# Pricing the planner from the trace: a two-layer hybrid trunk on one core

## The chip, the cores and the metric

The kernel runs on one core of one Trainium2 chip. Its time is device microseconds of one launch. Three runs of the kernel before took 2161.36, 2166.35 and 2168.34 us; the median is 2166.35 us. One further execution was taken by the hardware profiler and is the source of every row below.

## The reference

Two layers act on 512 tokens of width 1024, all in f32:

```python
for i in range(2):
    x = layer_norm(ALPHA*x + 0.5*swiglu(x, ffn1...))          # width 2816
    x = layer_norm(ALPHA*x + hybrid_mixer(x, positions, ...))
    ffn = 0.5*swiglu(x, ffn2...)
    ple = sigmoid(x @ ple_w_gate) * (p[i] @ ple_w_proj)
    x = layer_norm(ALPHA*x + ffn + ple)
```

`hybrid_mixer` projects x to 12 groups of columns and runs three kinds of heads beside each other: four of retention (rotary angles, decay by distance, a state per chunk), a gated linear recurrence over 384 channels behind a causal convolution of width 4, and six of gated delta rule (convolution, SiLU, unit-norm q and k, per chunk a triangular system, a state carried from chunk to chunk). Their outputs, normed and gated, meet in `w_out`.

## The kernel before

All matmuls of weights are split: an f32 operand is rounded to a high part (ScalarE, `act`), the residue is its low part (VectorE, `tt` with SUB), and three products of 128 rows by 256 or 512 columns replace one. All of these go through `mm` (L305). The feed-forward stages take their gate and up matrices by a scheme of seven block products in place of eight (`Unit`), in 256-column matmuls; the down matrices, `w_out` and the embedding use 512-column ones (`rows`). Weights come by DMA on SP's queue into four `raw` tiles; `step_one` splits the next ones ahead of use, up to 14 us of matmul time ahead (`TARGET`) in the feed-forward stages and 5 us in the mixer. In part of them the residue is made by an accumulating DMA that POOL issues (L436, `add_one`), once ScalarE has written the negated weight.

The order of everything is decided while the program is written, by a planner on the host. It keeps a clock for each engine, P, D, A and G for TensorE, VectorE, ScalarE and GpSimd (L218 to L256 and L692 state their prices in ns), and for every 64 elements of a tile the time at which they are ready. `spend` (called by every helper) adds an instruction's price to its engine's clock, behind its inputs, with a hop of 110 ns between engines.

Side work is written as generators, so-called threads: `norm` (layer norm and transposes; these are marked urgent), `decays`, `delta` (one per pair of heads and half of the tokens: normalise k, build the triangular matrix, six levels of its inverse, two rounds of refinement, states, output norm), `lru`, `turn` and `retention`, and `blocks`/`combine` for the sums of the seven-product scheme. After every main matmul `poll` looks at each thread:

```python
if th.t + HOP <= clk["P"] and (th.urgent or max(clk["D"], clk["A"]) <= p + BACKLOG) and not th.done:
    step(th)
```

So a thread's next step (some transposes or small matmuls and what VectorE, ScalarE and GpSimd do with them) is placed in the engines' queues once its last result is ready by the planner's clocks, and only while neither D nor A is more than `BACKLOG` ahead of P. `wait_until` steps threads, earliest first, when the main line can't go on: for a PSUM bank, or for free slots in SBUF. In the mixer `unit` does the main work: it waits for three free slots (five before a rotated block), takes weights, runs 24 matmuls of 512 columns, and convolves, rotates or applies a function. The blocks come in the order q (3), x (3), l (3), r (4), z (3), g (2), after the k and v blocks; each q block spawns a `delta` of the second half. Hardware queues run strictly in the order that results.

`either(ns_v, ns_g)` (L223) gives a product to GpSimd when that clock, plus ns_g, is earlier than VectorE's plus ns_v; the mixer's weight residues use it with 70 + 1.04 n against 90 + 2.0 n, masks with 600 against 1110. `pmm` and `ptr` are side matmuls and transposes, with prices given at each call (58, 107, 215 and others).

Of the kernel before, what the change touches and what calls it, by code (L numbers as in the profile page):

```python
# [25 lines left out]
TARGET = 14.0  # L26
LEVELS = (2, 4, 8, 16, 32, 64)
HOP = 110.0
BACKLOG = 1800.0
GUARD = 6  # L30
ROOM_D = 4
ROOM_1, ROOM_2, ROOM_3, ROOM_O, ROOM_R = 5, 4, 3, 2, 5
# [77 lines left out]
def tile_trunk(ctx: ExitStack, tc: tile.TileContext, a, out):  # L110
# [28 lines left out]
    def blocks(ap):  # L139
        per = ap.ap[0][0]  # L140
        lo = ap.offset % per
        hi = lo + sum((n - 1) * abs(k) for k, n in ap.ap[1:])
        name = ap.tensor.name
        return [(name, i) for i in range(lo // 64, hi // 64 + 1)]

    def available(e, ins):
        t = 0.0
        for ap in ins:
            for b in blocks(ap):
                if b in ready:  # L150
                    f, g = ready[b]
                    t = max(t, f + (60.0 if g == e else HOP))
        return t

    def place(e, t, ns):

        if e == "P" or INORDER:
            clk[e] = max(clk[e], t) + ns
            return clk[e]
        q = gaps[e]  # L160
        for i, (g0, g1) in enumerate(q):
            s = max(g0, t)
            if s + ns <= g1:
                del q[i]
                if g1 - s - ns > 50.0:
                    q.insert(i, (s + ns, g1))
                if s - g0 > 50.0:
                    if len(q) == q.maxlen:
                        q.popleft()
                        i -= 1  # L170
                    q.insert(max(i, 0), (g0, s))
                return s + ns
        s = max(ends[e], t)
        if s - ends[e] > 50.0:
            q.append((ends[e], s))
        ends[e] = s + ns
        return s + ns
# [13 lines left out]
    def spend(e, ns, outs=(), ins=()):  # L191
        c = cur[0]
        t = place(e, max(c.t0, available(e, ins)), ns)
        for ap in outs:
            for b in blocks(ap):
                ready[b] = (t, e)
        if e != "P":
            clk[e] = max(clk[e], t)
        if not lazy[0]:
            c.t = max(c.t, t)  # L200
        emitted[0] += 1
# [5 lines left out]
    def size(ap):  # L207
        n = 1
        for d in ap.shape[1:]:
            n *= d  # L210
        return n
# [3 lines left out]

    def act(out, in_, func=AF.Copy, **kw):
        nc.scalar.activation(out=out, in_=in_, func=func, **kw)  # L217
        ns = 60 + 0.833 * size(out) + 90 * len(kw)  # L218
        if tables.get(func, table[0]) != table[0]:
            table[0] = tables[func]  # L220
            ns += 1280
        spend("A", ns, [out], [in_] + [v for v in kw.values() if not isinstance(v, float)])
# [4 lines left out]

    def ew(eng, ns, n, out, *ins):
        if eng is nc.gpsimd:
            spend("G", 90 + 2.0 * n, [out], ins)  # L230
        else:
            spend("D", ns + 1.04 * n, [out], ins)

    def tt(out, in0, in1, op, eng=None):
        (eng or nc.vector).tensor_tensor(out=out, in0=in0, in1=in1, op=op)  # L235
        ew(eng, 70, size(out), out, in0, in1)

    def stt(out, in0, scalar, in1, op0, op1):
        nc.vector.scalar_tensor_tensor(out=out, in0=in0, scalar=scalar, in1=in1, op0=op0, op1=op1)  # L239
        ew(None, 100, size(out), out, in0, in1, *([] if isinstance(scalar, float) else [scalar]))  # L240

    def ts(out, in0, s1, op0, s2=None, op1=None, eng=None):
        if op1 is None:
            (eng or nc.vector).tensor_scalar(out=out, in0=in0, scalar1=s1, scalar2=None, op0=op0)  # L244
        else:
            (eng or nc.vector).tensor_scalar(out=out, in0=in0, scalar1=s1, scalar2=s2, op0=op0, op1=op1)
        ew(eng, 100, size(out) * 0.6, out, in0, *[x for x in (s1, s2) if x is not None and not isinstance(x, float)])

    def cp(out, in_, eng=None):
        (eng or nc.vector).tensor_copy(out=out, in_=in_)  # L250
        ew(eng, 70, size(out), out, in_)

    def rsum(out, in_):
        nc.vector.tensor_reduce(out=out, in_=in_, axis=AX.X, op=ALU.add)
        ew(None, 70, size(in_), out, in_)

    def pmm(out, lhsT, rhs, ns, start=True, stop=True):

# [7 lines left out]
    def step(th):  # L266
        keep = cur[0]
        cur[0] = th
        th.t0 = clk["P"]
        try:  # L270
            next(th.gen)
        except StopIteration:
            th.done = True
            side.remove(th)
        cur[0] = keep
# [7 lines left out]
    def poll():  # L283
        p = clk["P"]
        for th in list(side):
            if th.t + HOP <= clk["P"] and (th.urgent or max(clk["D"], clk["A"]) <= p + BACKLOG) and not th.done:
                step(th)
# [89 lines left out]
    for l in range(L):  # L377
        gu_at["ln_ffn1", l] = add_gu(l, a["wgu1"], GROUP)
        add_rows(a["ffn1_w_down"][l], MT)
        for c in (0, 804, 1608):  # L380
            n = min(804, 2144 - c)
# [63 lines left out]
    def low(hi, lo, w, dma, j):  # L445
        if dma and not any(th.urgent for th in side):
            act(lo, w, scale=-1.0)
            readers[j] += 1
            adds.append((cur[0].t, lo, w, j))
            cur[0].t += 6000.0  # L450
        else:
            tt(lo, w, f32(hi), SUB)
# [8 lines left out]
    def step_one():  # L461
# [7 lines left out]
        if c == "plain":  # L469
            w = ra[:, 0:n]  # L470
            hi = slots.get([128, 1024], F32R)
            lo = slots.get([128, 1024], F32R)
            act(hi[:, 0:n], w)
            tt(lo[:, 0:n], w, f32(hi[:, 0:n]), SUB, either(70 + 1.04 * n, 90 + 2.0 * n) if in_mixer[0] else None)
            readers[j] -= 1
            o = new_op((j,), [hi, lo], [("plain", hi, lo)], 5.4)
        elif c in ("P1", "P2"):
# [3 lines left out]
            for s in (slice(0, 512), slice(512, 1024)) if st["step"] < 3 else (slice(0, 1024),):  # L481
                act(hi[:, s], w[:, s])
                low(hi[:, s], lo[:, s], w[:, s], n, j + int(c == "P2"))
# [15 lines left out]
        elif c == "B2b":  # L499
            hi, lo = sums.pop(j)  # L500
            low(hi, lo, rb, n, j + 1)
            readers[j + 1] -= 1
            o = new_op((j,), [hi, lo], [(nm, hi[:, s], lo[:, s]) for nm, s in (("B21", slice(0, 512)), ("B22", slice(512, 1024)))], US)
        elif c == "sum1":
            t = sums[j] = slots.get([128, 2, 512], F32)
            tt(t[:, 0, :], ra[:, 512:1024], ra[:, 0:512], SUB)
            tt(t[:, 1, :], rb[:, 512:1024], t[:, 0, :], SUB)
            readers[j] -= 1
            readers[j + 1] -= 1
        elif c == "sum2":  # L510
            t = slots.get([128, 2, 512], F32)
            tt(t[:, 0, :], rb[:, 512:1024], ra[:, 512:1024], SUB)
            tt(t[:, 1, :], rb[:, 0:512], sums[j][:, 1, :], SUB)
            slots.put(sums[j])
            sums[j] = t
            readers[j] -= 1
            readers[j + 1] -= 1
        else:
            hi = slots.get([128, 2, 512], F32R)
            lo = slots.get([128, 2, 512], F32R)  # L520
            t = sums[j]
            act(hi, t)
            tt(lo, t, f32(hi), SUB)
            if c == "Tb":
                slots.put(sums.pop(j))
            o = new_op((j,), [hi, lo], [(nm, hi[:, i, :], lo[:, i, :]) for i, nm in enumerate(("T1", "T2") if c == "Ta" else ("T3", "T4"))], US)
# [156 lines left out]
    def rsqrt(dst, src, add, mul=None):  # L683

        if mul is None:
            ts(dst, src, add, ADD)
        else:
            ts(dst, src, mul, MUL, add, ADD)
        e = half_neg
        if len(dst.shape) == 2:  # L690
            e = e.to_broadcast(list(dst.shape))
        nc.gpsimd.tensor_tensor(out=dst, in0=dst, in1=e, op=POW)  # L692
        spend("G", 300 + 165 * size(dst), [dst], [dst])

    def new_xT():
        for kp in range(4):
# [8 lines left out]
    def norm(t, acc, c, gb, out=None, halves_done=None, kind="whole"):  # L705
# [6 lines left out]
        for h in range(2):  # L712
            while halves_done is not None and halves_done[0] <= h:
                yield
            s = slice(h * 512, (h + 1) * 512)
            stt(x[:, s], acc[h], c / ALPHA, x[:, s], MUL, ADD)
            ps.put(acc[h])
            if halves_done is not None:
                nc.vector.bn_stats(out=bs[:, h, :], in_=x[:, s])
# [8 lines left out]
        if halves_done is not None:  # L728
            for h in range(2):
                s = slice(h * 512, (h + 1) * 512)  # L730
                stt(x[:, s], x[:, s], mv[:, 0:1], gb[0][:, s], SUB, MUL)
                stt(x[:, s], x[:, s], rs, gb[1][:, s], MUL, ADD)
                nc.sync.dma_start(out=out[t * 128:(t + 1) * 128, s], in_=x[:, s])
            slots.put(gb[0], gb[1])
            return
# [1217 lines left out]
```

## Time and profile before

| what | us |
|---|---|
| median of three runs | 2166.35 |
| the profiled execution | 2159.74 |
| its span, first to last instruction | 2158.0 |
| TensorE busy in the span | 2115.7 |
| VectorE, ScalarE, GpSimd busy | 1417.5, 1114.7, 343.3 |
| mean granted clock of TensorE | 0.991 |

Busy time counts an instruction from its start to its end on the engine; matmuls overlap and their ends are modelled. The granted clock is a share of 2.4 GHz; at the lower of its two levels it is 0.5. Stages of the first layer, in us from the start of the span: feed-forward 0 to about 376, mixer to about 670, embedding to about 740, second feed-forward to about 1110. The second layer follows with the same pattern some 1071 us later.

### The profile page before, as it was taken

Reading aid. Unit: us, or ns where it says so; the run is one execution under the profiler, and the core shown is the slowest. Engines: PE = TensorE matmul, PEld = TensorE weight load, DVE = VectorE, ACT = ScalarE, POOL = GpSimd, SP = SyncE. Lnnn points to the kernel's source line nnn. Section 1 sums busy time; section 2 is a strip of 40 time slices with the busy share of each in tenths; the row PEclk is TensorE's granted clock in tenths of the full one; section 3 lists DMA queues with packets and bytes.
Section 4 is the critical chain, followed back from the end, with each engine's and each line's share of the span. In section 5 each row is a group of like instructions: output and inputs, shape, how many; then the busy total and the mean of one; then the engine's idle time right before and its main releaser. Section 6 shows DMA issues by size and latency. Waiting matters only on the chain.

```text
span 2158.0 us, 35722 instructions
## 1 busy us (share of the span) xinstructions
PE 2115.7 (98%) x14264; PEld 1905.0 (88%) x14264; DVE 1417.5 (66%) x2415; ACT 1114.7 (52%) x1880; POOL 343.3 (16%) x325
## 2 busy tenths in 40 slices
PE   8999999999999999999999999999999999999998
PEld 7999988977778899998899998889777889999986
DVE  7766636878767766673486665378787677666634
ACT  7666532657334666662266664335564247666530
POOL 3111001233221111100011110012333111111000
PEclk9999999999999999999999999999999999999999
DMA  9776532210133576763247765322102336766621
GB/s 283 178 177 171 162 118 79 79 47 11 59 115 113 127 173 165 176 179 115 83 117 172 174 169 164 106 84 69 38 21 66 98 113 146 187 167 165 182 88 40
DMA packets 104343, 268.38 MB, mean 124 GB/s; under 512 B 9328, under 2 KB 11376, under 8 KB 104176
## 3 DMA queue, kind: packets, MB, share of 16 engines
q1 hardware_dynamic: 80416, 201.07, 28.5%
q0 software_dynamic: 23760, 65.02, 16.8%
q8 instruction: 112, 1.84, 0.3%
q14 instruction: 55, 0.45, 0.1%
HBM read 198.95 MB, written 2.10 MB: 93 GB/s over the span
## 4 chain that ended last, share of the span: by engine, by line
PE 86%; DVE 7%; DMA 3%; ACT 2%; POOL 1%; issue 1%; SPq 0%; DVEq 0%; POOLq 0%; ACTq 0%
PE p L305 78%; PE p L259 6%; DVE s L235 4%; PE p L263 2%; DMA raw<-in_wgu_dram 1%; ACT s L217 1%; DMA s<-in_xT_dram 1%; DMA s<-raw 1%; POOL fs L692 1%; DVE s L239 1%; DMA raw<-in_win_fm_dram 0%; ACT L217 0%; DVE x L239 0%; DVE s L1404 0%; POOL s L235 0%
## 5 line engine op out<-in xcount | busy, mean ns | idle before, releaser
L305 PE MATMUL p<-s,s 128*128 128x256 f32 (+1 forms) x12048 | 1945.1, 320 | 14.0 <-ACT s L217 12.6
L305 PEld LDWEIGHTS p<-s,s 128*128 128x128 f32 x12048 | 1710.5, 191 | 170.6 <-ACT s L217 14.2
L217 ACT ACTIVATE s<-raw 128x1024 fp32r<-128x1024 f32 (+2 forms) x521 | 462.1, 911 | 316.9 <-PE p L305 235.4
L235 DVE TENSOR_TENSOR s<-s,s 128x1024 fp32r<-128x1024 f32 (+4 forms) x433 | 383.9, 908 | 182.7 <-ACT s L217 148.0
L217 ACT ACTIVATE s<-s 128x512 fp32r<-128x512 f32 (+5 forms) x485 | 336.6, 709 | 322.0 <-DVE s L235 164.8
L235 DVE TENSOR_TENSOR s<-raw,s 128x1024 fp32r<-128x1024 f32 (+3 forms) x351 | 334.5, 958 | 245.2 <-ACT s L217 191.6
L217 ACT ACTIVATE s<-p 128x256 f32<-128x256 f32 (+5 forms) x740 | 279.0, 407 | 316.2 <-PE p L305 121.7
L436 POOL DMA_DIRECT2D s<-raw x165 | 143.2, 872 | 881.2 <-ACT s L217 694.2
L235 DVE TENSOR_TENSOR s<-p,s 128x256 f32<-128x256 f32 (+4 forms) x376 | 157.1, 432 | 73.9 <-PE p L305 48.3
L259 PE MATMUL p<-s,s 128*128 128x128 f16 (+6 forms) x1496 | 154.2, 250 | 7.8 <-DVE s L235 6.7
L235 DVE TENSOR_TENSOR s<-raw 128x512 f32<-128x512 f32 x168 | 115.0, 686 | 68.7 <-PE p L305 65.0
L692 POOL TENSOR_TENSOR rs<-rs,half_neg 128x1 f32<-128x1 f32 x24 | 34.8, 1450 | 537.5 <-DVE rs L244 537.5
L259 PEld LDWEIGHTS p<-s,s 128*128 128x128 f32 (+1 forms) x680 | 89.9, 195 | 21.6 <-issue 6.3
L239 DVE SCALAR_TENSOR_TENSOR s<-p,vecs,s 128x255 f32<-128x255 f32 (+5 forms) x128 | 69.3, 550 | 19.7 <-PE p L263 14.8
L217 ACT ACT_TABLE_LOAD x48 | 61.6, 1283 | 14.5 <-DVE tails L250 7.2
L235 DVE TENSOR_TENSOR s<-s,p 128x512 fp32r<-128x512 f32 (+3 forms) x92 | 45.7, 502 | 16.6 <-PE p L259 12.9
L259 PEld LDWEIGHTS <-s 128*128 128x128 f16 x816 | 37.4, 101 | 20.7 <-issue 11.5
L235 DVE TENSOR_TENSOR s<-p,lvm 128x512 f16<-128x512 f32 x72 | 48.2, 683 | 10.6 <-PE p L259 10.2
L235 POOL TENSOR_TENSOR s<-s,cst 128x512 f32<-128x512 f32 x26 | 36.8, 1417 | 96.1 <-DVE s L235 70.0
L239 DVE SCALAR_TENSOR_TENSOR x<-p,x 128x512 f32<-128x512 f32 x48 | 31.5, 682 | 29.2 <-PE p L305 29.0
L263 PE MATMUL p<-cst,s 128*128 128x128 f32 x172 | 33.0, 290 | 9.6 <-ACT s L217 5.3
L263 PEld LDWEIGHTS p<-cst,s 128*128 128x128 f32 x172 | 20.5, 145 | 17.5 <-ACT s L217 6.1
(103 smaller groups left out, 663.3 us busy)
## 6 DMA issues: line engine op xcount, KB each, us to landing
raw<-in_wgu_dram SPq DMA_DIRECT2D x172, 512.0 KB, 4.6
raw<-in_ffn_w_down_dram SPq DMA_DIRECT2D x88, 512.0 KB, 3.6
s<-raw POOLq DMA_DIRECT2D x83, 512.0 KB, 5.4
raw<-in_win_fm_dram SPq DMA_DIRECT2D x48, 512.0 KB, 3.6
s<-raw POOLq DMA_DIRECT2D x82, 256.0 KB, 4.2
raw<-in_w_out_dram SPq DMA_DIRECT2D x16, 512.0 KB, 3.6
raw<-in_ple_w_gate_dram SPq DMA_DIRECT2D x16, 512.0 KB, 4.0
s<-in_xT_dram SPq DMA_DIRECT2D x4, 512.0 KB, 6.3
```

The lines of the kernel that those rows point to most:

```text
L217: nc.scalar.activation(out=out, in_=in_, func=func, **kw)
L235: (eng or nc.vector).tensor_tensor(out=out, in0=in0, in1=in1, op=op)
L239: nc.vector.scalar_tensor_tensor(out=out, in0=in0, scalar=scalar, in1=in1, op0=op0, op1=op1)
L259: nc.tensor.matmul(out=out, lhsT=lhsT, rhs=rhs, start=start, stop=stop)
L263: nc.tensor.transpose(out, in_, idn)
L305: nc.tensor.matmul(out=out, lhsT=lhsT, rhs=rhs, start=start, stop=stop, skip_group_check=resumed)
L436: nc.gpsimd.dma_start(out=out, in_=in_, accum_op=ADD)
L692: nc.gpsimd.tensor_tensor(out=dst, in0=dst, in1=e, op=POW)
```

## The change

The prices of ScalarE, VectorE and GpSimd instructions get new constants, and `BACKLOG` goes from 1800 to 4000 ns. Prices of TensorE, the hop, `either`'s figures and the prices that a few places give by themselves stay.

```diff
-BACKLOG = 1800.0
+BACKLOG = 4000.0
...
     def act(out, in_, func=AF.Copy, **kw):
         nc.scalar.activation(out=out, in_=in_, func=func, **kw)
-        ns = 60 + 0.833 * size(out) + 90 * len(kw)
+        ns = 180 + 0.84 * size(out) + 20 * len(kw)
...
         if eng is nc.gpsimd:
-            spend("G", 90 + 2.0 * n, [out], ins)
+            spend("G", 260 + 2.05 * n, [out], ins)
         else:
             spend("D", ns + 1.04 * n, [out], ins)
...
     def tt(out, in0, in1, op, eng=None):
-        ew(eng, 70, size(out), out, in0, in1)
+        ew(eng, 155, size(out), out, in0, in1)
...
     def stt(out, in0, scalar, in1, op0, op1):
-        ew(None, 100, size(out), out, in0, in1, ...)
+        ew(None, 155, size(out), out, in0, in1, ...)
...
     def ts(out, in0, s1, op0, s2=None, op1=None, eng=None):
-        ew(eng, 100, size(out) * 0.6, out, in0, ...)
+        ew(eng, 150, size(out) * 0.52, out, in0, ...)
...
     def cp(out, in_, eng=None):
-        ew(eng, 70, size(out), out, in_)
+        ew(eng, 150, size(out) * 0.52, out, in_)
...
     def rsum(out, in_):
-        ew(None, 70, size(in_), out, in_)
+        ew(None, 155, size(in_), out, in_)
...
     def rsqrt(dst, src, add, mul=None):
         nc.gpsimd.tensor_tensor(out=dst, in0=dst, in1=e, op=POW)
-        spend("G", 300 + 165 * size(dst), [dst], [dst])
+        spend("G", 1050 if size(dst) > 1 else 1400, [dst], [dst])
```

## Rows read from the trace of the kernel before

**Rows 1.** The page's first part: busy us, share of the span, instructions.
```profile
PE 2115.7 (98%) x14264; PEld 1905.0 (88%) x14264; DVE 1417.5 (66%) x2415; ACT 1114.7 (52%) x1880; POOL 343.3 (16%) x325
```

**Rows 2.** Windows by stage: stretch, its length, busy us (instructions) per engine, clock, DMA.
```profile
55.00:150.00 95.00, 95.00 (x777) 93.58 (x777) 67.62 (x113) 61.89 (x103) 15.73 (x19) 1.00 0.73 177
...
345.00:380.00 35.00, 35.00 (x222) 31.59 (x221) 29.95 (x59) 15.36 (x29) 6.94 (x5) 1.00 0.29 91
...
440.00:650.00 210.00, 200.51 (x1416) 162.92 (x1415) 158.04 (x332) 101.56 (x207) 61.10 (x53) 0.96 0.18 57
...
1070.00:1125.00 55.00, 53.26 (x399) 50.50 (x398) 49.43 (x79) 34.73 (x63) 6.37 (x6) 1.00 0.32 87
...
1520.00:1710.00 190.00, 181.62 (x1320) 148.68 (x1319) 143.97 (x303) 94.93 (x194) 56.54 (x49) 0.96 0.20 61
```

**Rows 3.** Groups by form, TensorE, 225 to 345 us: busy, mean ns, idle before.
```profile
L305 PE MATMUL p<-s,s 128*128 128x512 f32 x447 | 101.9, 389 | 0.0
L305 PE MATMUL p<-s,s 128*128 128x256 f32 x154 | 19.3, 284 | 0.0
```

**Rows 4.** Windows inside the mixers; engines PE, PEld, DVE, ACT, POOL.
```profile
475.00:508.00 33.00, 33.00 (x329) 27.47 (x329) 25.01 (x53) 21.66 (x53) 10.45 (x11) 1.00 0.06 18
508.00:533.00 25.00, 22.14 (x178) 17.98 (x177) 21.06 (x48) 19.11 (x38) 10.08 (x10) 0.86 0.00 1
1580.00:1605.00 25.00, 22.14 (x179) 18.08 (x178) 21.25 (x50) 19.59 (x39) 10.07 (x10) 0.86 0.00 1
```

**Rows 5.** Windows of line L305 alone (PE, PEld, clock, DMA) in the first mixer.
```profile
510.00:515.00 5.00, 0.00 (x0) 0.00 (x0) 1.00 0.00 0
515.00:520.00 5.00, 0.00 (x0) 0.00 (x0) 1.00 0.00 0
520.00:525.00 5.00, 0.00 (x0) 0.00 (x0) 0.73 0.01 3
525.00:530.00 5.00, 0.00 (x0) 0.00 (x0) 0.59 0.00 0
...
560.00:565.00 5.00, 1.54 (x5) 1.01 (x5) 0.82 0.01 3
...
635.00:640.00 5.00, 1.50 (x4) 1.28 (x5) 0.50 0.00 0
```

**Rows 6.** Time line of TensorE: start, us, instructions, idle before them and its releaser.
```profile
486.09 0.72 PE L259 MATMUL p<-s 64*128 64x128 f32 x8
...
520.61 0.44 PE L263 MATMUL p<-cst,s 128*128 128x128 f32 x2 [1.80 <-ACT s L217]
```

**Rows 7.** Groups by form, whole span, VectorE and ScalarE: busy, mean ns, idle.
```profile
L235 DVE TENSOR_TENSOR s<-raw,s 128x1024 fp32r<-128x1024 f32 x171 | 210.1, 1238 | 206.6 <-ACT s L217 163.3 <-issue 23.1 <-PE p L305 19.7
...
L235 DVE TENSOR_TENSOR s<-p,lvm 128x512 f16<-128x512 f32 x72 | 48.2, 683 | 10.6 <-PE p L259 10.2
...
L217 ACT ACTIVATE s<-raw 128x1024 fp32r<-128x1024 f32 x345 | 360.9, 1054 | 248.0 <-PE p L305 178.4 <-DVE s L235 19.3 <-PE p L259 9.1
...
L217 ACT ACTIVATE s<-p 128x256 f16<-128x256 f32 x120 | 38.8, 387 | 26.6 <-PE p L259 26.6
```

**Rows 8.** Groups by line, whole span: GpSimd, and small VectorE products.
```profile
L692 POOL TENSOR_TENSOR rs<-rs,half_neg 128x1 f32<-128x1 f32 x24 | 34.8, 1450 | 537.5 <-DVE rs L244 537.5
...
L235 POOL TENSOR_TENSOR s<-raw,s 128x1024 fp32r<-128x1024 f32 x8 | 20.2, 2522 | 25.5 <-PE p L305 16.9 <-ACT s L217 8.6
...
L692 POOL TENSOR_TENSOR ss<-ss,half_neg 128x8 f32<-128x8 f32 x4 | 6.5, 1634 | 30.5 <-DVE ss L246 30.5
...
L235 DVE TENSOR_TENSOR fs<-fs,rq 128x4 f32<-128x4 f32 x12 | 4.1, 341 | 11.4 <-POOL fs L692 11.4
...
L235 DVE TENSOR_TENSOR fs<-fs 128x4 f32<-128x4 f32 x12 | 1.9, 157 | 0.2
```

**Rows 9.** Time line of all engines near 512 us: start, us, instruction, idle before.
```profile
512.31 1.28 POOL L235 TENSOR_TENSOR s<-s,s 128x512 f32<-128x512 f32 x1
512.37 1.23 DVE L235 TENSOR_TENSOR fs<-fs,rq 128x4 f32<-128x4 f32 x1 [0.53 <-POOL fs L692]
```

More of the change, by code (lines that the diff above doesn't have):

```diff
@@ L235, in tt @@
         (eng or nc.vector).tensor_tensor(out=out, in0=in0, in1=in1, op=op)
-        ew(eng, 70, size(out), out, in0, in1)
+        ew(eng, 155, size(out), out, in0, in1)
     def stt(out, in0, scalar, in1, op0, op1):
         nc.vector.scalar_tensor_tensor(out=out, in0=in0, scalar=scalar, in1=in1, op0=op0, op1=op1)
-        ew(None, 100, size(out), out, in0, in1, *([] if isinstance(scalar, float) else [scalar]))
+        ew(None, 155, size(out), out, in0, in1, *([] if isinstance(scalar, float) else [scalar]))
     def ts(out, in0, s1, op0, s2=None, op1=None, eng=None):
@@ L246, in ts @@
             (eng or nc.vector).tensor_scalar(out=out, in0=in0, scalar1=s1, scalar2=s2, op0=op0, op1=op1)
-        ew(eng, 100, size(out) * 0.6, out, in0, *[x for x in (s1, s2) if x is not None and not isinstance(x, float)])
+        ew(eng, 150, size(out) * 0.52, out, in0, *[x for x in (s1, s2) if x is not None and not isinstance(x, float)])
     def cp(out, in_, eng=None):
         (eng or nc.vector).tensor_copy(out=out, in_=in_)
-        ew(eng, 70, size(out), out, in_)
+        ew(eng, 150, size(out) * 0.52, out, in_)
     def rsum(out, in_):
         nc.vector.tensor_reduce(out=out, in_=in_, axis=AX.X, op=ALU.add)
-        ew(None, 70, size(in_), out, in_)
+        ew(None, 155, size(in_), out, in_)
     def pmm(out, lhsT, rhs, ns, start=True, stop=True):
```

## Prediction

> **What bounds the kernel now.** I read the engine totals first. TensorE is busy 98% of a 2158.0 us span, so 42 us of it is idle; no other engine passes 66% [rows 1]. The table by stage says where those 42 us are. In a feed-forward stretch nothing is idle, 95.00 of 95 us, and at the joint of two stages 35.00 of 35 or 53.26 of 55. In the two mixers, 440 to 650 us and 1520 to 1710 us, TensorE lacks 9.5 and 8.4 us, its granted clock averages 0.96, and VectorE is busy 75% [rows 2]. The reader is to see that about 18 of the 42 us lie in two windows that fill a fifth of the span; most of the rest is the start, waiting for the first weights, and the tail after the last matmul.
>
> A busy share can hide waits, so I held the planner's TensorE prices against the paces of full stretches. 256-column matmuls go at 19.3/154 = 125 ns against 120 planned, 512-column ones at 101.9/447 = 228 against 218 (a few per cent of the records are missing) [rows 3]. The planner is right there, and the feed-forward stages run at TensorE's own pace.
>
> Then I cut the first mixer finer. From 475 to 508 us TensorE is full (33.00 of 33) and does 329 instructions, 10 per us; VectorE is busy 76%. From 508 to 533 us it does 178, 7 per us, at a clock of 0.86, with VectorE at 84%. The second layer repeats it, 179 at 0.86 [rows 4]. In the middle 20 us of that stretch no matmul of the main line L305 runs at all, and the clock falls to 0.59 in one 5 us piece [rows 5]: of the two levels, 2.4 and 1.2 GHz, it was at the lower most of the time, after TensorE had waited. I call this the starved stretch. The code says why: the rotated blocks call `unit`, which waits for five free slots, and the side threads hold them. What runs is side work alone, TensorE waiting in order on ScalarE (1.80 us at 520.61) [rows 6].
>
> Price of the starved stretch: at the pace of the 33 us before it, which includes the long L305 matmuls, its 178 instructions are 17.9 us, so at least 25 - 18 = 7 us per layer is lost. Ceiling for anything this change can give: per mixer about 9 us of idle time, and the time at the lower clock, (1 - clock) x 5 us summed over the pieces below full clock: 1.35, 2.05, 0.9 and 2.5 us in the four lowest [rows 5], about 7 us. Both layers: some 32 us, 1.5%.
>
> **The change part by part.** No instruction is added or removed, apart from the choice between VectorE and GpSimd that `either` makes from the planner's clocks. What changes is the order.
>
> *Durations.* A 512-element VectorE product was reckoned 70 + 1.04 x 512 = 602 ns, is now 687; the trace has 683. A 256-element ScalarE copy was 273, is now 395; the trace 387. A 1024-element scaled one was 1003, is now 1060; the trace 1054 [rows 7]. The one-element power was 465, is now 1400; the trace 1450. One goes the wrong way: eight elements, 1620 to 1050, while the trace has 1634, four instances [rows 8]. The new figures are truer, but TensorE's own side prices stay: `pmm` reckons 215 ns for each 64-row matmul, while eight of them take 0.72 us together [rows 6]. So the planner's TensorE time still runs too fast in side work.
>
> In the feed-forward stages this is worth nothing. The only things there that follow these clocks are the urgent norm threads and the accumulate DMAs, each issued 57 ns later by the planner against operands prepared up to 14 us ahead; the cover is a full TensorE, and without it each would show as a wait on L305, and in 95 us there is none [rows 2]. At the stage joints the norm's transposes move back by about 1.2 us of planner time (the power 0.9, the rest 50 to 90 each) behind other main work; between -2 and +2 us in all, taken as 0, since TensorE is full or nearly so in those pieces as well [rows 2].
>
> In a mixer a `delta` thread's next step is emitted once the planner thinks its last result is there. Per level of its inverse the reckoning grows by 85 ns on VectorE and 2 x 122 on ScalarE, six levels 2.0 us; normalisations, masks, solve and states add about 3.5 by the same differences. Each `delta` so advances 5.5 us later against main work. Does that cost? From 475 to 508 us TensorE was idle for nothing, so the old optimistic placing did not stall it there [rows 4], and later placing only leaves more side work for the starved stretch: 0 to +5.5 us per layer. Inside that stretch truer durations should put the readier thread first: of its 25 us, 2.9 are plain idle [rows 4], so 0 to -3 us per layer.
>
> *The gate.* A non-urgent thread steps only while neither VectorE's nor ScalarE's planned clock is more than BACKLOG ahead of TensorE's. After a q unit the old planner has ScalarE ahead by 576 (scaled copy) + 110 + 1891 (three conv taps) + 110 + 486 (SiLU) + 913 (next weights) = 4.1 us and VectorE, with the next weights' residue of 1135 and a hop, by 5.3. The gate of 1.8 is shut for 3.5 us of the next 5.4. With the new figures VectorE stands 5.9 ahead and a gate of 4.0 is shut for 1.9 us. The other kinds of unit come out 1.1 to 1.8 us better. Call it 1.7 us per unit; nine units (q, x, l) lie ahead of the starved stretch: 15 us per layer in which threads may step and could not. Not every thread has a step due then; half, 7.5 us, is my value, between 0 and 15.
>
> Against the later stepping, of which about half lies ahead of the starved stretch (2.7 us), side work comes some 4 to 5 us earlier there. TensorE is full where it goes, so the gain is only what the starved stretch loses now: side work moved out of a stretch at 7 per us into one at 10. Of the 7 us or more lost per layer I take 4, near the 4 to 5 that the steps come earlier, with bounds of +5.5 and -16 (all idle and low-clock time gone). Two layers: -8 us. The profiled execution took 2159.74 us, 1.74 of it outside the span, and would take 2151.7. The median shown is 2166.35, 6.6 above that execution, so the forecast against it is 2158.
>
> *POOL.* With VectorE's clock further ahead, `either` gives more products to GpSimd: a split goes there when VectorE is 1.0 us further ahead, and takes 2522 ns [rows 8] instead of 1238 [rows 7]. Eight do so now. The trace shows that this isn't free even for VectorE: a product of 4 elements took 1.23 us, from 512.37 to the end, within 0.02 us, of a GpSimd product begun at 512.31 [rows 9]; the twelve of its kind average 341 ns, and the like of it without such a neighbour 157 [rows 8]. The Trainium skill (SBUF — State Buffer, "SBUF: two separate sides") says that GpSimd and a VectorE operation with two SBUF inputs share one port pair under an exclusive lock, the later one blocking until the first ends. The trace agrees in that pair; by this rule each product sent to GpSimd also stops a VectorE one, which the planner does not reckon.
>
> **The rivals.**
> 1. *Nothing measurable.* The moved steps land in a TensorE that is full, and the five-slot wait ends when the last `delta` gives up its slots, whatever came before. For: both layers show the same 22.14 us of busy time in 25, as a chain with nothing to spare would [rows 4]. Against: the stretch's length is a chain of side steps, and that is what is moved. Between -6 and +6 us: 2166.
> 2. *Slower: the chains come later.* If the threads were held by their own last results and not by the gate, only the 5.5 us per `delta` acts. The place is the same, 508 to 533 us and its twin; each grows by 5.5 us and runs longer at the lower clock, about 2 us more: 2 x 7.5 = +15, 2181. It decides as soon as the gate was open for most due steps. For it: VectorE had 8 of 33 us free just before the stretch [rows 4], which a backlog gate alone would not leave. Against: the unit arithmetic above.
> 3. *Slower: GpSimd.* If eight more splits go to GpSimd, VectorE saves 8 x 1.2 us of its own and stands for up to 8 x 2.5: a net 10 us over two mixers in which it is 75 to 84% busy [rows 2, 4]. About half shows: +5, 2171; with a queue of 4 us ahead of the main line's splits, up to +10.
>
> **How the numbers follow.** A measurement tells about 0.3%, 6.5 us, from no change. Forecast (starved stretches shorter, 7 to 20 us in all) 0.42. Rival 1: 0.30. Rival 2: 0.17. Rival 3: 0.11, of which a little falls within the 0.3%. Faster 0.42, same 0.32, slower 0.26. The likeliest is 2158, its own range 2144 to 2160. The 8-in-10 range has to take in rival 2 with some of rival 3 on top, and a gain of most of the ceiling below: 2136 to 2186.
>
> **What would show it.** Right: in the profile after, the stretch without L305 matmuls in each mixer is shorter than 20 us, the mixer windows hold fewer idle us and a clock nearer 1.0, VectorE is above 76% in the 30 us before it, and the feed-forward windows are unchanged to 1 us. Rival 2 would show a longer one with VectorE less busy before it; rival 3 more than eight splits of 1024 on GpSimd and more small VectorE products over 1 us. I am wrong altogether if the time moves in the feed-forward stages or the joints.

## The result: 1.0% slower, all of it in the two mixers

The changed kernel takes 2186.14 us (median of four runs) beside 2163.86 for the kernel before: ratio 1.0102, 95% interval 1.0068 to 1.0136. The forecast was 2158, its range 2136 to 2186. All profiles below are of one execution each; the changed kernel's is the fastest of its four, 2181.1 us.

First the totals of the kernel after, then its windows by stage (stretch, length, busy us and instructions of PE, PEld, DVE, ACT, POOL, clock, DMA share, GB/s).

```profile
PE 2122.2 (97%) x14264; PEld 1910.3 (88%) x14264; DVE 1402.7 (64%) x2403; ACT 1117.2 (51%) x1880; POOL 363.0 (17%) x337
```

```profile
55.00:150.00 95.00, 95.00 (x780) 93.81 (x780) 64.96 (x106) 61.92 (x103) 15.47 (x18) 1.00 0.72 176
345.00:380.00 35.00, 34.47 (x220) 30.97 (x219) 30.75 (x63) 15.64 (x31) 5.83 (x5) 1.00 0.29 92
...
440.00:650.00 210.00, 194.21 (x1359) 158.55 (x1358) 149.76 (x321) 104.14 (x207) 67.73 (x57) 0.96 0.19 60
1080.00:1135.00 55.00, 53.63 (x407) 51.11 (x404) 49.51 (x78) 34.88 (x63) 5.78 (x6) 1.00 0.37 98
1520.00:1730.00 210.00, 194.98 (x1367) 159.12 (x1364) 150.26 (x322) 104.59 (x208) 67.91 (x56) 0.95 0.19 60
```

TensorE did the same 14264 instructions. The feed-forward window is as before and the joints are within 0.5 us of it [rows 2]; the first mixer's window has 15.8 us idle where it had 9.5. To place the whole loss I measured, to about 0.1 us, each stretch from the first 268-column matmul (start of a mixer) to the first 256-column one of the next feed-forward stage, in us:

| | first ffn | mixer + embedding | next two ffn | mixer + embedding | last ffn | span |
|---|---|---|---|---|---|---|
| before | 365.2 | 368.2 | 703.3 | 366.9 | 354.5 | 2158.0 |
| after | 364.3 | 377.7 | 703.4 | 378.0 | 355.9 | 2179.3 |

So 9.5 + 11.1 = 20.6 of the 21.3 us are mixer and embedding. Summed over 5 us pieces of these stretches, TensorE's idle time went from 10.2 to 17.8 and from 9.5 to 16.7 us, and the time lost to the lower clock, (1 - granted clock) x 5 us a piece, from 8.5 to 8.5 and from 8.5 to 10.2. That is 7.6 of the 9.5 us and 8.9 of the 11.1; the rest lies in busy time.

The starved stretch is twice as long. The windows around it, and L305 alone in 5 us pieces (PE, PEld, clock, DMA):

```profile
440.00:494.00 54.00, 52.33 (x407) 38.49 (x406) 34.75 (x65) 37.38 (x71) 23.82 (x21) 1.00 0.12 38
494.00:540.00 46.00, 39.25 (x397) 35.24 (x395) 37.75 (x81) 33.60 (x79) 11.11 (x15) 0.88 0.01 1
```

```profile
490.00:495.00 5.00, 4.41 (x17) 2.54 (x15) 1.00 0.00 0
495.00:500.00 5.00, 0.00 (x0) 0.00 (x0) 0.86 0.02 3
500.00:505.00 5.00, 0.00 (x0) 0.00 (x0) 0.50 0.00 0
505.00:510.00 5.00, 0.00 (x0) 0.00 (x0) 0.61 0.00 0
...
525.00:530.00 5.00, 0.00 (x0) 0.00 (x0) 1.00 0.02 3
530.00:535.00 5.00, 0.73 (x2) 0.30 (x2) 1.00 0.00 0
535.00:540.00 5.00, 0.57 (x1) 0.19 (x1) 0.96 0.00 0
```

The main line stops at 494 us in place of 509 [rows 5] and goes on at 540 in place of 532: 46 us with three L305 matmuls. In them TensorE is idle 6.75 us; in the 54 us before, VectorE is busy 64%, where it was 76% [rows 4].

It would be natural to say that main work ran ahead of side work. The counts say otherwise. From the start of the mixer to the stop of the changed kernel, and in the kernel before to the same point of the main line, all engines and then L305 alone (the first two pairs are of the kernel before, to that point and to its own stop):

```profile
365.19:489.22 124.03, 122.96 (x960) 107.04 (x958) 102.03 (x235) 72.80 (x143) 35.66 (x27) 1.00 0.22 68
365.19:489.22 124.03, 106.54 (x602) 86.26 (x600) 1.00 0.22 68
...
365.19:508.62 143.43, 142.36 (x1142) 123.24 (x1141) 116.79 (x266) 84.65 (x171) 41.07 (x33) 1.00 0.19 59
365.19:508.62 143.43, 116.06 (x625) 90.61 (x623) 1.00 0.19 59
...
364.30:494.77 130.47, 126.82 (x958) 107.45 (x957) 100.71 (x233) 80.29 (x150) 46.07 (x35) 1.00 0.19 64
364.30:494.77 130.47, 107.89 (x601) 86.52 (x599) 1.00 0.19 64
```

With the same main work both have done the same number of side instructions, 358 and 357, the changed kernel 6.4 us later. Of that 2.6 us are idle time, and part of the rest is longer kinds of side instructions. So much of the first mixer's 9.5 us has come before the starved stretch, and the second mixer is alike (about 6 of 11.1 us). Then the changed kernel stops, while the kernel before takes one more block of 24 main matmuls and stops at 509 us with 517 side instructions done. The stop comes after nine blocks of 24 (q, x, l), and the first rotated one is next, so by the code the five-slot wait falls on the first rotated block after the change and on the second before it, and what is left for the stretch is 384 side instructions in place of 167. Why the slots are short one block earlier, the profile doesn't show.

A time line of TensorE shows what it waits for in the stretch, and the lists of its waits over the whole span (total us, times, longest; three lines of the kernel after, then three of the kernel before) show which waits have grown:

```profile
534.15 0.73 PE L305 MATMUL p<-s,s 128*128 128x512 f32 x2
534.72 2.40 PE L259 MATMUL p<-s,s 128*128 128x128 f32 x16
538.79 0.71 PE L259 MATMUL p<-s,s 64*128 64x128 f32 x4 [1.66 <-DVE s L235]
```

```profile
PE p L263 <- DVE s L235: 13.0, 8, 2.6
PE p L305 <- ACT s L217: 11.2, 7, 7.6
PE p L259 <- DVE s L235: 10.5, 14, 1.7
...
PE p L305 <- ACT s L217: 12.6, 6, 7.4
PE p L259 <- DVE s L235: 8.8, 6, 1.7
...
PE p L263 <- DVE s L235: 3.8, 9, 0.9
```

L305's wait for ScalarE is mostly the start of the kernel, as before. What has grown is the wait of side transposes (L263) for VectorE's results, from 3.8 to 13.0 us; that of side matmuls (L259) was there before.

GpSimd got twice the weight splits, 16 for 8 [rows 8], at 2647 ns each (groups by line: busy, mean ns, idle before):

```profile
L235 POOL TENSOR_TENSOR s<-raw,s 128x1024 fp32r<-128x1024 f32 x16 | 42.3, 2647 | 102.3 <-ACT s L217 101.8 <-issue 0.6
...
L235 DVE TENSOR_TENSOR fs<-fs,rq 128x4 f32<-128x4 f32 x12 | 2.0, 163 | 10.8 <-POOL fs L692 10.8
```

### The profile page after: what moved, and what is told of

Read it like the earlier page. It is cut to its first block, busy times and chain, and to the rows that moved or that the text cites. A ratio compares the mean times of both kernels' runs of the same rounds, so it can differ in the third digit from the quotient of the medians.

```text
span 2179.3 us, 35725 instructions
## 1 busy us (share of the span) xinstructions
PE 2122.2 (97%) x14264; PEld 1910.3 (88%) x14264; DVE 1402.7 (64%) x2403; ACT 1117.2 (51%) x1880; POOL 363.0 (17%) x337
## 4 chain that ended last, share of the span: by engine, by line
PE 84%; DVE 7%; DMA 3%; ACT 3%; POOL 1%; issue 1%; SPq 0%; DVEq 0%; ACTq 0%; POOLq 0%
PE p L305 77%; PE p L259 5%; DVE s L235 5%; DMA raw<-in_wgu_dram 2%; ACT s L217 2%; PE p L263 1%; DMA s<-in_xT_dram 1%; ACT L217 0%; DVE s L239 0%; POOL rq L692 0%; DMA raw<-in_win_fm_dram 0%; POOL fs L692 0%; DVE x L239 0%; DVE s L1404 0%; POOL rs L692 0%
## 5 line engine op out<-in xcount | busy, mean ns | idle before, releaser
L305 PE MATMUL p<-s,s 128*128 128x256 f32 (+1 forms) x12048 | 1939.8, 320 | 14.0 <-ACT s L217 11.2
L305 PEld LDWEIGHTS p<-s,s 128*128 128x128 f32 x12048 | 1713.4, 191 | 174.9 <-ACT s L217 13.7
L235 DVE TENSOR_TENSOR s<-raw,s 128x512 f32<-128x512 f32 (+3 forms) x343 | 321.3, 944 | 248.3 <-ACT s L217 189.4
L259 PE MATMUL p<-s,s 128*128 128x64 f16 (+6 forms) x1468 | 153.4, 251 | 9.1 <-DVE s L235 7.0
L259 PEld LDWEIGHTS p<-s,s 128*128 128x128 f32 (+1 forms) x652 | 88.6, 198 | 23.4 <-issue 7.5
L239 DVE SCALAR_TENSOR_TENSOR s<-p,vecs,s 128x255 f32<-128x255 f32 (+4 forms) x128 | 69.0, 551 | 9.4 <-ACT s L217 8.6
L235 DVE TENSOR_TENSOR s<-s,p 128x128 f32<-128x128 f32 (+3 forms) x92 | 45.4, 502 | 27.8 <-PE p L259 23.8
L235 POOL TENSOR_TENSOR s<-raw,s 128x1024 fp32r<-128x1024 f32 x16 | 42.3, 2647 | 102.3 <-ACT s L217 101.8
L235 DVE TENSOR_TENSOR s<-p,lvm 128x512 f16<-128x512 f32 x72 | 47.7, 685 | 15.0 <-PE p L259 14.5
L259 PEld LDWEIGHTS <-s 128*128 128x128 f16 x816 | 38.6, 101 | 16.1 <-issue 11.8
L263 PE MATMUL p<-cst,s 128*128 128x128 f32 x172 | 32.6, 288 | 11.3 <-DVE s L235 9.7
```

What stands on the lines that cost most here:

```text
L259: nc.tensor.matmul(out=out, lhsT=lhsT, rhs=rhs, start=start, stop=stop)
L263: nc.tensor.transpose(out, in_, idn)
L305: nc.tensor.matmul(out=out, lhsT=lhsT, rhs=rhs, start=start, stop=stop, skip_group_check=resumed)
```

## Experiments

Ratios are to the kernel before on the same chip. "Mixers" is the length of the two mixer-and-embedding stretches; "idle" and "clock" are TensorE's idle time and the time lost to the lower clock in them, as above; "no L305" sums the 5 us pieces of one mixer without a main matmul (us). The ratio comes from all runs of a kernel, the other columns from its one profiled execution. In seven of these (e3, e4, n1, n2, d_old108, d_new108, d_new112) another 3.6 to 6.5 us lie ahead of the first mixer, which begins at 368.8 to 371.7 us in place of 365.2.

| kernel | prices | gate | else | ratio, 95% interval | mixers | idle | clock | no L305 |
|---|---|---|---|---|---|---|---|---|
| before | old | 1800 | | 1 | 368.2, 366.9 | 10.2, 9.5 | 8.5, 8.5 | 20, 20 |
| after | new | 4000 | | 1.0102, 1.0068 to 1.0136 | 377.7, 378.0 | 17.8, 16.7 | 8.5, 10.2 | 30, 30 |
| e1_gate | old | 4000 | | 1.0072, 1.0045 to 1.0098 | 373.3, 372.1 | 13.3, 14.5 | 8.5, 5.1 | 15, 15 |
| e2_prices | new | 1800 | | 1.0226, 1.0201 to 1.0251 | 394.7, 393.7 | 23.1, 24.3 | 18.8, 17.1 | 40, 40 |
| e3_nopool | new | 4000 | no splits on GpSimd | 1.0050, 1.0031 to 1.0070 | 375.3, 377.6 | 13.8, 13.3 | 8.5, 11.9 | 45, 45 |
| e4_early | new | 4000 | steps 500 ns earlier | 1.0082, 1.0061 to 1.0103 | 375.7, 375.8 | 13.7, 13.9 | 12.0, 12.0 | 10, 10 |
| n1_old_open | old | none | | 1.0240, 1.0218 to 1.0262 | 393.7, 395.3 | 22.1, 21.7 | 20.4, 23.9 | 10, 10 |
| n2_new_open | new | none | | 1.0079, 1.0058 to 1.0100 | 381.8, 380.5 | 13.7, 14.7 | 18.8, 17.1 | 20, 25 |
| p_act | ScalarE new | 1800 | | 1.0083, 1.0051 to 1.0116 | 381.8, 381.8 | 10.6, 10.9 | 23.9, 23.9 | 30, 30 |
| p_dve | VectorE new | 1800 | | 1.0113, 1.0092 to 1.0134 | 380.9, 380.0 | 15.4, 15.8 | 17.1, 15.3 | 40, 40 |
| c_1700 | old | 1700 | | 1.0093, 1.0066 to 1.0120 | 375.0, 378.1 | 16.2, 15.2 | 8.5, 13.7 | 45, 45 |
| c_1900 | old | 1900 | | 1.0077, 1.0053 to 1.0102 | 377.8, 381.5 | 15.2, 14.6 | 10.2, 15.3 | 40, 45 |
| c_hop112 | old | 1800 | hop 112 | 1.0148, 1.0119 to 1.0176 | 386.5, 386.1 | 14.6, 14.4 | 20.4, 20.5 | 45, 40 |
| c_a3800 | new | 3800 | | 1.0067, 1.0041 to 1.0093 | 374.4, 379.7 | 13.5, 12.9 | 10.2, 17.1 | 20, 25 |
| d_old108 | old | 1800 | hop 108 | 1.0109, 1.0085 to 1.0133 | 382.3, 382.1 | 17.5, 17.5 | 15.4, 15.3 | 35, 35 |
| d_old1820 | old | 1820 | | 1.0101, 1.0080 to 1.0122 | 377.0, 382.4 | 17.6, 15.2 | 8.5, 18.8 | 35, 30 |
| d_new108 | new | 4000 | hop 108 | 1.0114, 1.0080 to 1.0149 | 375.7, 380.7 | 17.4, 15.6 | 6.8, 13.6 | 30, 30 |
| d_new112 | new | 4000 | hop 112 | 1.0060, 1.0044 to 1.0076 | 374.8, 376.0 | 15.5, 16.4 | 8.6, 8.5 | 30, 30 |

**The two halves of the change.** My theory was the prediction's second rival, L: later stepping. Its rivals: the gate, G, and the splits on GpSimd, P.

```diff
# e1_gate, against before          # e2_prices, against after
-BACKLOG = 1800.0                  -BACKLOG = 4000.0
+BACKLOG = 4000.0                  +BACKLOG = 1800.0
```

> The kernel before with the gate alone opened, 1800 to 4000; prices as before. Theory L (later stepping: the new prices put each side step later in TensorE's queue, main work runs ahead, and the stretch without L305 matmuls grew from 23 to some 45 us per mixer; the gate is not to blame): the gate alone is no slower than before, 2155 to 2168, and its stretch without L305 is 23 us or shorter. Theory G (the gate: a queue of up to 4 us on VectorE ahead of the main line): 10 us or more slower than before, 2174 and up, with 12 to 16 weight splits on GpSimd.

> The changed kernel with the gate back at 1800: new prices alone. Theory L: slower than before by as much as the whole change or more (the gate's opening works against the loss), 2180 to 2200, the stretch without L305 about 45 us or longer. Theory G: within 6 us of before. Theory P (the share of weight splits on GpSimd): the time follows the number of 128x1024 splits on GpSimd, 8 in the kernel before, 16 in the changed one.

Measured: +0.72% and +2.26%, 2178.88 and 2213.6 us, which fits none of them whole. The gate alone costs, against L; the prices alone cost twice the whole change, so with the new prices the wider gate gives back more than half, as L had it. The splits on GpSimd, 8 before, 10 in e1, 16 after and 18 in e2, have the order of the times, as P had it, but two more of them go with 0.7% at one end and 1.2% at the other. The runs further down break the order: hop 112 has 8 and costs 1.48%, p_dve has 20 and costs 1.13% (groups by line, one line of each).

```profile
L235 POOL TENSOR_TENSOR s<-raw,s 128x1024 fp32r<-128x1024 f32 x8 | 19.2, 2397 | 21.9 <-ACT s L217 21.1 <-PE p L305 0.9
L235 POOL TENSOR_TENSOR s<-raw,s 128x1024 fp32r<-128x1024 f32 x20 | 49.3, 2463 | 52.3 <-ACT s L217 43.2 <-PE p L305 9.1
```

In e1 ScalarE also loads its tables 66 times, where the kernels before and after load 48 times (groups by line, the load in e1):

```profile
L217 ACT ACT_TABLE_LOAD x66 | 84.7, 1283 | 19.8 <-DVE s L239 9.5 <-DVE sp L239 4.9 <-DVE sp L235 3.8
```

**The splits, and the lateness, taken away from the changed kernel.**

```diff
# e3_nopool
-            tt(lo[:, 0:n], w, ..., SUB, either(...) if in_mixer[0] else None)
+            tt(lo[:, 0:n], w, ..., SUB)
# e4_early
-            if th.t + HOP <= clk["P"] and ...
+            if th.t + HOP - (0.0 if th.urgent else 500.0) <= clk["P"] and ...
```

> The changed kernel with the mixer's weight residues all on VectorE (no choice of GpSimd for them). Theory P: 8 to 15 us faster than the changed kernel, 2171 to 2178. Theory L: within 6 us of the changed kernel, the stretch without L305 still over 35 us.

> The changed kernel with each non-urgent side step admitted 500 ns of planner time earlier (the hop of 110 becomes -390 in the test of poll). Theory L: 8 to 20 us faster than the changed kernel, near the kernel before (2165 to 2178), and the stretch without L305 is back near 25 us. Theory P or G: within 6 us of the changed kernel or slower, since TensorE waits in its queue for steps not ready.

e3 came out at 2174.29 us, in P's band, some 11 us below the changed kernel by the two ratios; the intervals just overlap. Its profile can't say where the gain lies: it is of the slowest of its seven executions, 2182.63 us, the other six taking 2173.55 to 2175.42. Nor does the time prove P: the edit also gives another order, and d_new112 and c_a3800, further down, come out as low (1.0060, 1.0067) with 16 and 18 splits. Inconclusive, and at most part of the loss. e4 did what L asked of the stretch, 10 us without L305 in place of 30, and yet its time is 2182.58. The starved stretch is not the cost by itself: what e4 saved there it lost to the lower clock, 12.0 us for 8.5 and 10.2, and its idle time is still 13.7.

**No gate, and one price at a time.**

```diff
# n1_old_open, against before      # n2_new_open, against after
-BACKLOG = 1800.0                  -BACKLOG = 4000.0
+BACKLOG = 1.0e9                   +BACKLOG = 1.0e9
# p_act: before with the new price in act alone
# p_dve: before with the new prices in tt, stt, ts, cp and rsum alone
```

> Old prices, the gate taken away (BACKLOG 1e9). The gate alone at 4000 cost 13 us. Theory W (opening the gate costs by itself, as side work goes ahead of main work on VectorE and ScalarE): as slow as at 4000 or slower, 2175 to 2195. Theory C (the order is what it is, and any shift of it costs about the same; the kernel before sits in a good spot): anywhere from 2165 to 2185, with no order in the gate's width.

> New prices, the gate taken away. New prices cost 48 us with the gate at 1800 and 20 at 4000. Theory S (the new prices do harm by shutting the gate: planned VectorE and ScalarE clocks stand further ahead): without a gate they cost nothing more than old prices without a gate, so within 6 us of that run. Theory L (they do harm by later admission of each side step): 10 us or more above the run of old prices without a gate.

> The kernel before with the ScalarE price alone set new, gate at 1800. All new prices at 1800 gave 2213.6, +48 us. If the gate's shutting does it, a price counts by how much it moves the clock that stands furthest ahead; VectorE is the busier, so ScalarE's price alone gives +5 to +15 us, VectorE's alone +20 to +40. If later admission does it, ScalarE's gives as much as VectorE's, since 2 x 122 ns of each level's 329 are ScalarE's: +20 to +30.

> The kernel before with the VectorE prices alone set new, gate at 1800. If the gate's shutting does it: +20 to +40 us. If later admission does it: +10 to +20 us. If neither, and any change of order costs: +5 to +15 us, like the gate alone.

In these runs a wider gate is worse with old prices, 1, 1.0072, 1.0240, though 1900, further down, costs as much as 4000. With new prices it is better: 1.0226, 1.0102, 1.0079, the last step within the intervals. For the old prices W holds in direction and undershoots. For the new ones S looked for about the time of the run of old prices without a gate and L for a longer one, and it is 35 us below that: neither is the whole cause. Part of what n1 loses is seen in TensorE's waits, side matmuls standing before VectorE's and ScalarE's results; that they were queued too early is my reading.

```profile
PE p L263 <- DVE s L235: 21.0, 11, 3.7
PE p L305 <- ACT s L217: 17.6, 7, 7.3
PE p L259 <- ACT s L217: 7.5, 8, 2.8
PE p L263 <- DVE s L239: 7.5, 3, 3.5
```

One price at a time cost 21 and 24 us by the medians. ScalarE's lies in the band of later admission (+20 to +30), VectorE's in that of the gate (+20 to +40): the two runs point to opposite stories, and p_act's five executions spread from 2171.55 to 2192.99 us. That a part of the change costs as much as the whole made me suspect that any change would.

**Moves that mean nothing.**

```diff
# c_1700, c_1900, d_old1820: BACKLOG = 1700.0, 1900.0, 1820.0 in the kernel before
# c_hop112, d_old108: HOP = 112.0, 108.0 in the kernel before (110.0)
# c_a3800: BACKLOG = 3800.0, d_new108, d_new112: HOP = 108.0, 112.0 in the kernel after
```

> The kernel before with the gate at 1700 in place of 1800, a change of 6% that means nothing physical. Theory C (each order is a draw: the kernel before is a good draw among orders of which most lie 8 to 25 us higher, so any change of a constant costs about what this one did): 2172 to 2190. Theory M (the loss follows from how far the prices and the gate were moved, and small moves do little): within 6 us of before.

> The kernel before with the gate at 1900. Theory C: 2172 to 2190. Theory M: within 6 us of before, or a fifth of what 4000 cost (13 us) at the most.

> The kernel before with the planner's hop at 112 ns in place of 110, 2 ns on each hand-over. Theory C: 2172 to 2190. Theory M: within 4 us of before.

> The changed kernel with the gate at 3800 in place of 4000. Theory C: a new draw, anywhere from 2165 to 2205, and as likely as not over 6 us from the changed kernel. Theory M: within 6 us of the changed kernel, 2180 to 2192.

Theory M falls at the first three: 0.93, 0.77 and 1.48% for moves of 6% in the gate and 2 ns in the hop, the last beyond even C's band. The neighbour of the changed kernel, at 0.67% and 2179.15 us, is 7 us below it by the medians, inside C's band and just outside M's. How 2 ns become 34 us is seen in the order in which TensorE's instructions stand, hop 112 (+) against 110 (-): the first difference is one pair of side matmuls, one place later, near the 2080th row of the list (which has a row for each run of like instructions); some thirty rows further on the two lists part.

```diff
 L305 MATMUL p_83_4428<-s_317_3650,s_342_4110 128x512
-L259 MATMUL p_84_4451<-s_345_4198,cvr 128x512 x2
 L305 MATMUL p_83_4428<-s_318_3651,s_342_4110 128x512
+L259 MATMUL p_84_4452<-s_345_4198,cvr 128x512 x2
 L305 MATMUL p_83_4428<-s_317_3650,s_343_4111 128x512
```

In its profile the starved stretch is as long as the changed kernel's, and VectorE has slack ahead of it too (42.03 of 60, 70%), without one price moved. It begins a block later than in the changed kernel, where it began in the kernel before, with 442 side instructions done in place of 517. All engines, then L305 alone:

```profile
440.00:500.00 60.00, 58.28 (x492) 44.36 (x492) 42.03 (x78) 35.06 (x78) 15.81 (x15) 1.00 0.11 34
500.00:550.00 50.00, 44.65 (x369) 37.21 (x367) 42.80 (x94) 32.20 (x69) 20.64 (x21) 0.83 0.00 1
```

```profile
500.00:550.00 50.00, 3.03 (x7) 1.26 (x7) 0.83 0.00 1
```

**Do truer prices draw better orders?** Two more moves beside each kernel.

> The kernel before with the hop at 108 ns: a draw with old prices beside the gate of 1800. Theory C1 (orders under either set of prices are draws from about the same spread, 8 to 34 us above the kernel before): 2172 to 2198. Theory C2 (truer prices make the draws better on the mean, and the kernel before is an outlier of the worse set): higher than the mean of the new-price draws, 2180 to 2200.

> The kernel before with the gate at 1820: the smallest move of the gate tried. Theory C1: 2172 to 2198; C2: 2180 to 2200. If it stays within 6 us of before, the good spot has some width after all.

> The changed kernel with the hop at 108 ns: a draw with new prices beside the gate of 4000. Theory C1: 2172 to 2198. Theory C2: 2165 to 2186, like 4000 and 3800 so far.

> The changed kernel with the hop at 112 ns: a second such draw. Theory C1: 2172 to 2198. Theory C2: 2165 to 2186.

Old prices near 1800: 1.0093, 1.0077, 1.0148, 1.0109, 1.0101, mean 1.0106. New prices near 4000: 1.0102, 1.0067, 1.0114, 1.0060, mean 1.0086. The bands overlap and a difference of 0.2% between such means can't be told from none: C1 stands, C2 isn't shown.

One of the nine is no new draw. d_new108 is nearly the changed kernel itself: of the 13846 matmuls and transposes in the two written programs six stand in another place, and no instruction of VectorE, ScalarE or GpSimd does. It repeats the changed kernel's time on another chip (1.0114 and 1.0102), and its profile the starved stretches, 39.4 and 37.5 us without any L305 matmul in both kernels. So a move of the hop by 2 ns need not change the order, and in this one case where it doesn't, the time stays.

All nine are slower than the kernel before, and so are the other eight. Outside their spread lie e3, just below it, and e2 and n1, far above: a gate too tight for the new prices and none for the old. There gate and price seem to matter beyond the draw, by one kernel each. That all seventeen are slower would also follow if 1800 and 110 had been chosen by measured times; how they were chosen isn't on record.

## Why the prediction was wrong

- **What bounds the kernel** held: in the changed kernel's profile the feed-forward stages and joints moved by at most 1.4 us, and the time moved in the mixers, through idle time around the starved stretch and, in the second, the lower clock.
- **The step that failed is the sum of the gate and the later stepping**: "side work comes some 4 to 5 us earlier there", -4 us per layer with bounds of -16 and +5.5. It measured +9.5 and +11.1. The sum kept the starved stretch where it was and moved side work out of it. In the run no side work had been moved ahead by the time the main line stopped (357 side instructions for 358 at the same main work), that point came 6.4 us later, and the five-slot wait fell one block earlier, with 384 side instructions left for the stretch in place of 167.
- Why the new order is worse stays open. A move of a few us along a fixed order is not what a small change of a constant makes: with old prices each of five moves, of 2 ns of hop or 20 to 100 ns of gate, costs 0.8 to 1.5%. Where the order stays, in d_new108, the time stays too.
- The unit arithmetic had the right sign for what the gate does under the new prices, by one pair of orders: from 1800 to 4000 gave back 27 us (2213.6 and 2186.14, runs of different sets). It did not say what the new prices cost at 1800: 48 us, where "0 to +5.5 us per layer" was allowed.
- **Rival 1** (within 6 us) gave as its reason that the stretch's length is fixed by a chain. It went from 23 to 46 us.
- **Rival 2** named the side, the place and nearly the price (+15, measured +22), and both of its marks were met: a longer stretch, VectorE less busy before it. That is luck as far as its cause goes. Side steps did not come later against main work, hop 112 has the same marks without a price moved, and admitting the steps 500 ns earlier removed the stretch and not the loss.
- **Rival 3** was right that eight more splits go to GpSimd, and its second mark came too: of 378 VectorE instructions on at most 12 elements 11 take over 1 us, where 7 did. The twelve that averaged 341 ns [rows 8] now average 163, but others stand instead (kernel before, then after):

```profile
L246 DVE TENSOR_SCALAR fs<-fs 128x4 f32<-128x4 f32 x12 | 2.0, 163 | 0.2
L246 DVE TENSOR_SCALAR fs<-fs 128x4 f32<-128x4 f32 x12 | 6.3, 526 | 0.1
```

  In all, the 378 took 118.8 us in place of 115.7, so the price there is 3 us of VectorE's time. Its busy time in the two mixer stretches fell from 284.1 and 284.4 us to 276.2 and 275.7, no less than the eight splits given away are worth. What the splits cost beside that isn't settled: e3, with none, lost half as much, by another order.
- The rival that was missing is a property of the kernel before: it is the best of its neighbourhood, from which each of the five small moves tried costs 0.8 to 1.5%.
- The 8-in-10 range ended 0.14 us below the measured time. Its top was worked out from rival 2 with some of rival 3, so that nearness says nothing for the forecast, which had the sign wrong.

What stays open is what makes this order better than its neighbours. It has the least idle time of all (10.2 and 9.5 us; the next is p_act with 10.6 and 10.9) and a low clock loss, but no single mark, neither the starved stretch nor the splits, orders the runs. Whether the five-slot wait is what multiplies small differences wasn't tried.

## What to carry to other kernels

Before explaining what a change of a planner's constant did, move the same constant, or an unrelated one, by a meaningless amount and see how far the time goes. If that is as far as the change went, the change has not been measured, only drawn; several draws on each side are needed to tell prices apart, and the written orders are to be compared first, since a move can leave the order as it was. Before saying that one kind of work ran ahead of another, count both at the same point. And a better-calibrated planner is not a faster program while the order it writes turns on a few ns: a good order that was found is better kept as an order than as the constants that happen to give it.

## What the runs showed of the hardware

The lower clock is a cost of its own, and it varies between stretches that do the same work: in c_a3800 the two mixers agree in idle time to 0.6 us (13.5, 12.9), while the clock took 10.2 us of one and 17.1 of the other, and the second is 5.3 us longer.

It also varies between executions. The six of d_new108 run from 2175.39 us at a mean granted clock of 0.994 to 2200.76 at 0.982; 0.012 of the span is 26 us, and the two differ by 25.4. So a loss to the clock read from one profile is that of one execution.

And the sum of idle time doesn't tell it. p_act's profile has hardly more idle time in the mixers than that of the kernel before (10.6 and 10.9 us for 10.2 and 9.5) and lost 23.9 us to the clock in each, where the other lost 8.5; its five executions have clocks of 0.976 to 0.985, the twelve of the kernel before beside them 0.986 to 0.993. Most of it is one stretch, 612 to 649 us and its twin in the second layer. Around its start, from 605 to 615 us, TensorE waits for 1.5 us; then it counts as busy throughout, with side instructions, under 4 per us, and eight main matmuls in 30 us; full speed came back after main matmuls had started again. All engines, then L305 alone:

```profile
620.00:625.00 5.00, 5.00 (x19) 4.20 (x18) 0.57 (x2) 0.18 (x2) 0.00 (x0) 0.50 0.34 105
650.00:655.00 5.00, 5.00 (x24) 4.15 (x23) 4.41 (x8) 1.69 (x3) 0.88 (x1) 1.00 0.60 210
```

```profile
615.00:645.00 30.00, 4.54 (x8) 2.47 (x9) 0.50 0.22 70
645.00:650.00 5.00, 5.00 (x14) 3.58 (x12) 0.57 0.02 3
```

All eleven small VectorE instructions that take over 1 us in the changed kernel end within 0.05 us of a GpSimd product that they ran beside, those with one tile as their input too. One of four elements, of a kind that averaged 163 ns before, took 2.35 us next to a split on GpSimd that began 0.09 us before it:

```profile
635.30 2.35 DVE L246 TENSOR_SCALAR fs<-fs 128x4 f32<-128x4 f32 x1
635.21 2.40 POOL L235 TENSOR_TENSOR s<-raw,s 128x1024 fp32r<-128x1024 f32 x1 [4.39 <-ACT s L217]
```
